# A two-layer mixer block on one core: the output gate's rows are made beside the attention

## The chip, the cores and the metric

The kernel runs on one core of one Trainium2 chip. Its engines are TensorE (in the profile PE for matmuls and PEld for weight loads), VectorE (DVE), ScalarE (ACT), GpSimd (POOL) and SyncE (SP), whose queue issues the transfers. The metric is the device time of one execution in microseconds (us), lower is better; given is the median of several runs.

## What is computed

Two layers of a block with 1024 latent tokens and 256 context tokens of width 1024. In each layer the tokens are normalised and modulated, projected, and pass four mixers (two kinds of attention, a state-space scan, a long convolution); the concatenated mixers are projected by `w_out`, normalised, scaled and added to the input:

```python
out_l = jnp.concatenate([a_l, g_l, s_l, y_l], axis=-1) @ w_out[l]
x = x + gt_l * rms_norm(out_l, g_post[l])
if need_ctx:                                  # layer 0 alone
    out_c = jnp.concatenate([a_c, g_c, s_c, y_c], axis=-1) @ w_out[l]
    ctx = ctx + gt_c * rms_norm(out_c, g_post[l])
```

`gt_l` and `gt_c` are the gate thirds of a modulation, `silu(c) @ w_mod[l] + b_mod[l]`, one row of 1024 numbers each. The kernel works with the product of gate and norm weight, `gt * g_post`, spread over the 128 partitions: one such row set for the latent tokens, and in layer 0 a second for the context tokens.

## The kernel before

The program is unrolled: two layers, each with filters and in-projection, scan and convolution, attention, out-projection. A planner orders the instructions of each engine's queue by program order and by when it expects their inputs, and gives each pool of tiles its memory; pools are stacked from the left or from the right side of the memory, and a new pool may take the place of one that was closed (with waits for the tiles that it overlaps). Matrix products are made as three products of halves with full rate: high by high, high by low, low by high (`whi`, `wlo`, `omh`, `oml`, `owh`, `owl`, and so on); a gate row is one product in full fp32.

The attention (`attention`) walks over units of one head and 256 queries: 40 in layer 0 (four pairs of heads, five query blocks, the last of them context), 32 in layer 1. Its instructions on TensorE, VectorE, ScalarE and GpSimd keep the order of the string `ORDER`, software-pipelined over units. The last step of each round, `X`, calls `pump()`, from the round of the first unit up to one round after the last unit. A call runs the products that the call before left in `self.later`, in the attention's fixed order, and then takes one more step of the generator `side`, whose instructions are outside the fixed order:

```python
late, self.later = self.later, []
for f in late:
    f()
self.token = None
more = next(side, self)
...
while pump():        # behind the last round
    pass
```

`side` (in `dit_kernel`) first makes the gate blocks of the modulation (`mod_gates`, 8 steps; they are stored to a DRAM tensor, `self.mg`, in the profile modg), in layer 0 then the modulation of layer 1 (`mod_next`, 16 steps), then opens the pool `wo` on the right side and loads and splits the out-projection's weights (`out_weights`, 16 steps, loads of [128, 512] under the tag `owr` with four buffers in the attention's pool). Each modulation step leaves four small products in `self.later`; they write a PSUM tile `mps` of the tag `f`, which the attention's transposes use too.

After the attention the pool `op` opens on the left side, in layer 0 above the pool `hp` of the next layer's inputs, in layer 1 at its bottom. At its head stand the gate rows: `gate_rows` loads the four partial rows from modg and the bias (`mg`, 5 x 1024), loads the norm's weight to all partitions (`gt`, 512 KB), sums and spreads the rows by two products into a PSUM tile (`gps`, of the tag that the scores and the out-projection use too), and multiplies (`gt`). Then `outproj` runs over tiles of 128 tokens (10 in layer 0, 8 in layer 1): it loads the mixers' output (`omx`, from mixD, which the attention's units store to) and their gates (`ogt`, from gD), multiplies them on VectorE, splits (`omh` on ScalarE, `oml` on GpSimd), makes 48 products `ops`, takes the square sum on ScalarE and `ors` from it, multiplies `ops`, `ors` and `gt` on VectorE into `oy`, adds the residual `oxt` on GpSimd and stores. In layer 0 each pair of tiles is also normalised for layer 1 (`xps`, `h`, `hh`, `hl`). At the last tile the pool `wo` is closed; after layer 0 the pool `wp` of layer 1's in-projection weights (`wraw`, `whi` on ScalarE, `wlo` on GpSimd, products `ipc`) opens on the right side, where `wo` lay.

All loads and stores are issued by SP's queue in order (line 201); TensorE's products come from line 224, transposes from line 253.

Of the kernel before, what the change touches and what calls it, by code (L numbers as in the profile page):

```python
# [11 lines left out]
F32 = mybir.dt.float32  # L12
# [8 lines left out]
ADD, SUB, MUL = ALU.add, ALU.subtract, ALU.mult  # L21
# [166 lines left out]
class K:  # L188
# [201 lines left out]
                    self.later.append(partial(put, blk, ms))  # L390
                yield

    def gate_rows(self, l, which, P, gD):

        A = self.A
        mg = P.tile([5, 1024], F32, tag="oy", name="mg", bufs=4)
        self.load(mg[0:4, :], gD)
        self.load(mg[4:5, :], A["b_modg"][l])
        g = P.tile([128, 1024], F32, tag="gt", name="gt", bufs=2)
        self.load(g, A["g_post"][l].partition_broadcast(128))  # L400
        ps = self.b2("gps")
        for h in range(2):
            self.mm(ps[:, h * 512:(h + 1) * 512], self.sel[:, which:which + 1].to_broadcast([5, 128]),
                    mg[:, h * 512:(h + 1) * 512])
        self.tt(g, ps, g, MUL)
        return g


    def load_x(self, dst, i):
# [1407 lines left out]
def dit_kernel(ctx: ExitStack, tc: tile.TileContext, A, out):  # L1817
    k = K(tc, A, out)
# [5 lines left out]
    for l in range(2):  # L1824
        need = l == 0
        n = 1280 if need else 1024
# [17 lines left out]
        with k.pool("fil", side="right") as F, k.pool("pol") as Q:  # L1844
# [42 lines left out]
            for c in SCRIPT[l]:  # L1887
                if c in blocks:
                    x = blocks[c]
# [44 lines left out]
        def side(R):  # L1934
            with k.pool("ma", side="right") as M:
                gates, cols = [(l, 4), (l, 5)], [(1, b) for b in range(4)] if l == 0 else []
                steps = partial(k.mod_steps, M, k.mod_feed(M, gates + cols))
                yield from k.mod_gates(l, steps)
                if cols:
                    yield from k.mod_next(1, steps, M)  # L1940
            O = wo.enter_context(k.pool("wo", side="right"))
            yield from k.out_weights(l, O, R)


        with k.pool("att") as W, k.pool("asl") as L, k.pool("ast") as P:
            k.attention(l, (W, L, P), n, side(W))
        w = k.wo
# [7 lines left out]
        with k.pool("op") as P:  # L1955
            def getx(t, i):
                if l == 0:
                    k.load_x(t, i)
                else:
                    k.load(t, xD[:, i])  # L1960

            def putx(t, i):
                k.store(xD[:, i] if l == 0 else ot[i], t)

            tiles = range(10 if need else 8)
            gt = [k.gate_rows(l, x, P, k.mg) for x in range(2 if need else 1)]
            xns = []
            for i in tiles:
                y, ps = k.outproj(l, P, i, w, gt[i // 8], getx, putx)
                if i == tiles[-1]:  # L1970
                    wo.close()
                if l == 0:
                    k.xn_tile(P, y, y, ps)
                    xns.append(y)
                    if len(xns) == 2:
                        k.norm_cols(P, (i - 1, i), xns, *k.mod, k.hh, k.hl)
                        xns = []
# [22 lines left out]
```

## Time and profile before

| | |
|---|---|
| runs, median of 3 | 2194.62 us (2193.89 to 2198.0) |
| the profiled execution | 2194.1 us |
| its span, first to last instruction | 2192.3 us |
| TensorE busy (matmuls) | 1937.6 us, 88% |
| VectorE busy | 1593.3 us, 73% |
| GpSimd busy | 992.0 us, 45% |
| ScalarE busy | 916.5 us, 42% |
| mean granted TensorE clock | 0.927 |

The attention of layer 0 lies at about 726 to 1066 us of the span, its out-projection at 1066 to 1217, layer 1's attention at 1820 to 2078, its out-projection from 2078 to the end. In a timeline row stand the start in us, the time from the first start to the last end of the merged instructions, the engine, the line, the operation, what is written and read, the count, and in brackets the engine's idle time ahead of it with what ended it. SPq rows are transfers being issued; their landing shows in who waits for them.

### The profile page before, as it was taken

The numbers are of one execution on the slowest core, as the hardware profiler recorded it, in microseconds if no ns is written. First come the engines' busy times: TensorE is split into PE (matmuls) and PEld (weight loads), VectorE is DVE, ScalarE is ACT, GpSimd is POOL, SyncE is SP. The second block draws the span as 40 slices with busy tenths as digits, with TensorE's granted clock in tenths as the row PEclk, the third lists the DMA queues.
The fourth block names the chain that finished last, engine by engine and source line by source line (L and its number), as shares of the span: only waits on it lengthen the run. The fifth ranks groups of instructions, "written<-read, shape, count | busy, mean of one in ns | idle before, by whom it ended". The sixth has DMA issues, their size and how long they took to land.

```text
span 2192.3 us, 31534 instructions
## 1 busy us (share of the span) xinstructions
PE 1937.6 (88%) x10811; PEld 1617.4 (74%) x10811; DVE 1593.3 (73%) x2982; ACT 916.5 (42%) x1958; POOL 992.0 (45%) x798
## 2 busy tenths in 40 slices
PE   5788998789899899999799998997989949999888
PEld 2577887678778777788577776886767737899866
DVE  8799439855896589789444598389577858999732
ACT  4421233224334467667322322343233317788611
POOL 3757225564661244432155557246675622340034
PEclk7798899899999899999799987998999979999989
DMA  6323365337765546352343423264357673551053
GB/s 222 115 88 119 129 203 142 92 115 212 237 186 183 159 127 180 101 149 69 114 156 113 151 100 144 86 232 145 98 173 221 202 231 100 137 159 54 21 176 131
DMA packets 261249, 316.55 MB, mean 144 GB/s; under 512 B 46655, under 2 KB 203583, under 8 KB 257762
## 3 DMA queue, kind: packets, MB, share of 16 engines
q1 hardware_dynamic: 261090, 314.55, 47.0%
q8 instruction: 85, 1.39, 0.3%
q14 instruction: 74, 0.61, 0.1%
HBM read 207.61 MB, written 106.86 MB: 143 GB/s over the span
## 4 chain that ended last, share of the span: by engine, by line
PE 44%; DVE 29%; DMA 10%; issue 6%; POOL 5%; SPq 3%; ACT 2%; POOLq 0%; DVEq 0%; ACTq 0%
PE ipc L224 8%; PE apo L224 7%; PE ops L224 6%; PE aS L224 6%; PE apt L253 6%; DVE lU L233 3%; DVE sD L233 3%; SPq L201 3%; PE acx L224 2%; DVE sp L233 1%; PE mps L224 1%; DMA aq<-gP 1%; DVE aPl L233 1%; DVE lX L233 1%; PE fdft L224 1%
## 5 line engine op out<-in xcount | busy, mean ns | idle before, releaser
L224 PE MATMUL ipc<-hh,whi 128*128 128x512 f32 (+2 forms) x992 | 386.6, 390 | 18.8 <-DVE rs L512 6.9
L224 PE MATMUL ipc<-hl,whi 128*128 128x512 f32 (+2 forms) x992 | 380.9, 384 | 1.6 <-POOL hl L233 1.6
L224 PE MATMUL ipc<-hh,wlo 128*128 128x512 f32 (+2 forms) x992 | 379.8, 383 | 0.3 <-POOL wlo L233 0.3
L233 DVE TENSOR_TENSOR aPl<-apt,aPh 128x512 fp32r<-128x512 f32 x328 | 224.0, 684 | 20.9 <-ACT aPh L1663 17.0
L1663 ACT CAST aPh<-apt 128x512 fp32r<-128x512 f32 x328 | 186.5, 590 | 123.4 <-PE apt L253 115.4
L233 POOL TENSOR_TENSOR wlo<-wraw,whi 128x512 fp32r<-128x512 f32 x108 | 162.6, 1510 | 161.2 <-ACT whi L453 158.5
L224 PEld LDWEIGHTS ipc<-hh,whi 128*128 128x128 f32 x992 | 196.4, 198 | 51.9 <-DVE rs L512 7.9
L224 PEld LDWEIGHTS ipc<-hh,wlo 128*128 128x128 f32 x992 | 196.3, 198 | 30.9 <-issue 1.8
L224 PEld LDWEIGHTS ipc<-hl,whi 128*128 128x128 f32 x992 | 196.8, 198 | 29.9 <-POOL hl L233 2.3
L253 PE MATMUL apt<-ident,aP 128*128 128x128 f32 x1312 | 190.6, 276 | 1.0 <-DVE aPl L233 1.0
L224 PE MATMUL aS<-kst,aq 128*128 128x512 f32 x512 | 153.7, 423 | 20.5 <-DMA aq<-gP 14.9
L1628 DVE TENSOR_REDUCE am<-aS 128x1 f32<-128x1024 f32 x128 | 155.6, 1216 | 15.0 <-PE aS L224 15.0
L1691 POOL COPY aLB<-am 128x128 f32<-128x128 f32 x72 | 21.0, 291 | 313.6 <-DVE am L1683 313.6
L246 ACT ACTIVATE aP<-aS,am,rs 128x1024 f32<-128x1024 f32 x128 | 155.6, 1215 | 15.3 <-DVE am L243 14.2
L253 PEld LDWEIGHTS apt<-ident,aP 128*128 128x128 f32 x1312 | 149.1, 141 | 14.8 <-DVE aPl L233 6.4
L224 PE MATMUL apo<-aPh,vst 128*128 128x256 f32 x656 | 138.2, 308 | 14.9 <-ACT aPh L1663 9.0
L224 PE MATMUL apo<-aPl,vst 128*128 128x256 f32 x656 | 123.8, 286 | 3.0 <-DVE aPl L233 2.9
L224 PEld LDWEIGHTS apo<-aPh,vst 128*128 128x128 f32 x656 | 96.4, 190 | 29.9 <-DVE aob L233 14.8
L453 ACT CAST whi<-wraw 128x512 fp32r<-128x512 f32 x124 | 75.4, 618 | 101.9 <-PE ipc L224 56.6
L224 PEld LDWEIGHTS aS<-kst,aq 128*128 128x128 f32 x512 | 88.7, 194 | 35.5 <-issue 15.8
L224 PE MATMUL ops<-owh,omh 128*128 128x512 f32 x288 | 94.4, 408 | 19.4 <-ACT omh L1776 13.6
L224 PEld LDWEIGHTS apo<-aPl,vst 128*128 128x128 f32 x656 | 100.3, 190 | 10.0 <-DVE aPl L233 5.3
(368 smaller groups left out, 4485.7 us busy)
## 6 DMA issues: line engine op xcount, KB each, us to landing
wraw<-in_w_col_dram SPq DMA_DIRECT2D x64, 256.0 KB, 2.9
mraw<-in_w_mod_dram SPq DMA_DIRECT2D x32, 512.0 KB, 5.3
kst<-mK SPq DMA_DIRECT2D x16, 640.0 KB, 10.8
omx<-mixD SPq DMA_DIRECT2D x18, 512.0 KB
ogt<-gD SPq DMA_DIRECT2D x18, 512.0 KB, 4.6
wraw<-in_w_mod_dram SPq DMA_DIRECT2D x32, 256.0 KB, 4.0
k<-kt SPq DMA_DIRECT2D x16, 512.0 KB
lk<-k SPq DMA_DIRECT2D x8, 1024.0 KB, 6.1
```

The lines of the kernel that those rows point to most:

```text
L201: return self.nc.sync.dma_start(out=out, in_=in_)
L224: self.keep(self.nc.tensor.matmul(out, lhsT, rhs, start=start, stop=stop))
L233: self.keep((eng or self.nc.vector).tensor_tensor(out=out, in0=a, in1=b, op=op))
L246: self.keep(self.nc.scalar.activation(out=out, in_=in_, func=func, **k))
L253: self.keep(self.nc.tensor.transpose(out, in_, self.ident[:p, :p]))
L453: self.nc.scalar.copy(hi, raw)
L1628: self.keep(nc.vector.tensor_reduce(out=x["m"][:, 2 + qi:3 + qi], in_=x["S"][qi], axis=AX.X, op=ALU.max))
L1663: self.keep(nc.scalar.copy(h, ps))
L1691: self.keep(nc.gpsimd.tensor_copy(x["LB"][:, :, o:o + 64], x["m"][:, 10:12].unsqueeze(2).to_broadcast([128, 2, 64])))
```

## The change

`gate_rows` becomes a part of `side`, behind `out_weights`. The rows are tiles of the pool `wo` now, one for each of `n` row sets (two in layer 0, one in layer 1), and are made in halves of 512 columns. Each half loads its piece of modg and of the bias into a buffer of the tag `owr`, and leaves one product of TensorE and one of VectorE in `self.later`, with a PSUM tile of the tag `f`. The head of the out-projection has no gate rows any more, and its pool has no tiles `gt` and `mg`.

```diff
-    def gate_rows(self, l, which, P, gD):
+    def gate_rows(self, l, n, P, R):
 
         A = self.A
-        mg = P.tile([5, 1024], F32, tag="oy", name="mg", bufs=4)
-        self.load(mg[0:4, :], gD)
-        self.load(mg[4:5, :], A["b_modg"][l])
-        g = P.tile([128, 1024], F32, tag="gt", name="gt", bufs=2)
-        self.load(g, A["g_post"][l].partition_broadcast(128))
-        ps = self.b2("gps")
-        for h in range(2):
-            self.mm(ps[:, h * 512:(h + 1) * 512], self.sel[:, which:which + 1].to_broadcast([5, 128]),
-                    mg[:, h * 512:(h + 1) * 512])
-        self.tt(g, ps, g, MUL)
-        return g
+        self.gt = []
+        for which in range(n):
+            g = P.tile([128, 1024], F32, name=f"gt{which}")
+            self.load(g, A["g_post"][l].partition_broadcast(128))
+            self.gt.append(g)
+            for h in (slice(0, 512), slice(512, 1024)):
+                mg = R.tile([5, 512], F32, tag="owr", name="mg", bufs=4)
+                self.load(mg[0:4, :], self.mg[:, h])
+                self.load(mg[4:5, :], A["b_modg"][l][:, h])
+
+                def put(which=which, g=g, h=h, mg=mg):
+                    ps = self.f("gps")
+                    self.mm(ps, self.sel[:, which:which + 1].to_broadcast([5, 128]), mg)
+                    self.tt(g[:, h], ps, g[:, h], MUL)
+
+                self.later.append(put)
+                yield
...
             yield from k.out_weights(l, O, R)
+            yield from k.gate_rows(l, 2 if need else 1, O, R)
...
-            gt = [k.gate_rows(l, x, P, k.mg) for x in range(2 if need else 1)]
             xns = []
             for i in tiles:
-                y, ps = k.outproj(l, P, i, w, gt[i // 8], getx, putx)
+                y, ps = k.outproj(l, P, i, w, k.gt[i // 8], getx, putx)
```

## Rows read from the trace of the kernel before

**Rows 1.** The page, part 4: shares of the chain that ended last, by engine.

```profile
PE 44%; DVE 29%; DMA 10%; issue 6%; POOL 5%; SPq 3%; ACT 2%; POOLq 0%; DVEq 0%; ACTq 0%
```

**Rows 2.** Windows: stretch, length, busy us of PE, PEld, DVE, ACT, POOL, clock, DMA.

```profile
1080.00:1217.00 137.00, 125.38 (x546) 99.37 (x545) 57.75 (x96) 37.79 (x64) 76.19 (x53) 0.96 0.44 138
...
1820.00:2078.00 258.00, 253.48 (x1790) 226.25 (x1789) 238.71 (x431) 204.50 (x438) 59.22 (x76) 1.00 0.36 96
...
2091.00:2192.00 101.00, 91.53 (x384) 73.12 (x383) 31.47 (x37) 15.64 (x23) 43.34 (x24) 0.96 0.46 146
```

**Rows 3.** Timeline of SP's queue, end of layer 0's attention.

```profile
1014.43 1.90 SPq L201 DMA_DIRECT2D aq<-mS  x4
1029.51 30.28 SPq L201 DMA_DIRECT2D mixD<-aob  x3
1059.84 0.33 SPq L201 DMA_DIRECT2D mg<-modg  x1
...
1066.76 0.35 SPq L201 DMA_DIRECT2D mixD<-aob  x1
...
1068.88 0.61 SPq L201 DMA_DIRECT2D ogt<-gD  x1
```

**Rows 4.** Timeline of all engines, head of layer 0's out-projection.

```profile
1065.71 7.39 PE L224 MATMUL gps<-mg,sel 5*128 5x512 f32 x8
...
1077.02 1.36 DVE L236 SCALAR_TENSOR_TENSOR omx<-omx,ogt 128x512 f32<-128x512 f32 x3 [6.27 <-DMA ogt<-gD]
...
1078.41 1.04 ACT L1776 CAST omh<-omx 128x1024 fp32r<-128x1024 f32 x1 [12.66 <-DVE omx L236]
...
1079.51 1.22 PE L224 MATMUL ops<-owh,omh 128*128 128x512 f32 x2 [6.42 <-ACT omh L1776]
```

**Rows 5.** Timeline of all engines, head of layer 1's out-projection.

```profile
2078.59 0.28 SPq L201 DMA_DIRECT2D mg<-modg  x1
...
2079.27 0.36 SPq L201 DMA_DIRECT2D gt<-in_g_post_dram  x1
2079.80 0.55 SPq L201 DMA_DIRECT2D omx<-mixD  x1
...
2080.76 2.78 PE L224 MATMUL gps<-mg,sel 5*128 5x512 f32 x4 [3.84 <-DMA mg<-in_b_modg_dram]
...
2088.18 1.36 DVE L236 SCALAR_TENSOR_TENSOR omx<-omx,ogt 128x512 f32<-128x512 f32 x3 [3.12 <-DMA ogt<-gD]
...
2090.68 1.22 PE L224 MATMUL ops<-owh,omh 128*128 128x512 f32 x2 [7.14 <-ACT omh L1776]
```

**Rows 6.** Timeline of all engines, from layer 0's last tile to layer 1's in-projection.

```profile
1214.30 6.69 SPq L201 DMA_DIRECT2D wraw<-in_w_col_dram  x4
...
1218.11 2.53 POOL L233 TENSOR_TENSOR wlo<-wraw,whi 128x512 fp32r<-128x512 f32 x2
...
1218.18 1.28 DVE L236 SCALAR_TENSOR_TENSOR oy<-ops,ors,gt 128x1024 f32<-128x1024 f32 x1 [2.11 <-POOL ors L233]
...
1219.45 0.80 PE L224 MATMUL ipc<-hh,wlo 128*128 128x512 f32 x1 [0.26 <-POOL wlo L233]
...
1220.57 2.41 POOL L233 TENSOR_TENSOR oy<-oy,oxt 128x1024 f32<-128x1024 f32 x1
```

**Rows 7.** Windows around layer 0's gate products and its first tile.

```profile
1068.90:1072.40 3.50, 3.50 (x5) 1.16 (x4) 1.23 (x1) 0.00 (x0) 0.00 (x0) 0.50 0.64 207
...
1084.90:1087.00 2.10, 2.10 (x10) 1.68 (x10) 0.00 (x0) 0.65 (x1) 1.37 (x1) 0.96 0.60 167
```

**Rows 8.** Timeline of POOL in layer 1's attention: its copy comes once a unit.

```profile
1847.11 0.29 POOL L1691 COPY aLB<-am 128x128 f32<-128x128 f32 x1 [2.17 <-DVE am L1683]
...
1881.62 0.29 POOL L1691 COPY aLB<-am 128x128 f32<-128x128 f32 x1 [2.17 <-DVE am L1683]
...
1929.63 0.29 POOL L1691 COPY aLB<-am 128x128 f32<-128x128 f32 x1 [1.52 <-DVE am L1683]
...
1945.18 0.29 POOL L1691 COPY aLB<-am 128x128 f32<-128x128 f32 x1 [1.75 <-DVE am L1683]
```

## The prediction

> **What bounds the kernel now.** I read the chain of work that ended last first: TensorE carries 44% of it, VectorE 29%, waits for transfers 10% [rows 1]. The kernel has several stages with different limits, so I split the span next. In the layer-1 attention TensorE is busy 253.5 us of 258 and VectorE 238.7; in the out-projection of layer 0 TensorE is busy 125.4 us of 137, in that of layer 1 91.5 of 101 [rows 2]. All three are bound by TensorE, so an instruction added to its stream in the attention costs its full time, and a head start of an out-projection is kept to its end. What the change touches is the few microseconds before an out-projection's first product. There the reader is to look at which wait ends last. In layer 0 the first product `ops` starts at 1079.51, after the cast omh at 1078.41, after the VectorE product that waited until 1077.02 for the load ogt [rows 4]; this load was issued on SP's queue at 1068.88, behind the loads of both gate rows, and landed 8.1 us later [rows 3]. In layer 1 it is the same: VectorE is released by ogt at 2088.18, first product at 2090.68 [rows 5]. The gate products themselves (gps) end before ogt lands and stand on no path: 1073.1 against 1077.0 in layer 0, 2083.5 against 2088.2 in layer 1 [rows 4, 5]. So what the change can win is not the products but their loads, which stand ahead of ogt on SP's queue and share the transfer engines with it.
>
> **What the change does, part by part.** The number of TensorE records of the gate rows stays at 12. The VectorE products become 6 halves instead of 3 wholes, the loads 15 instead of 9 (five for each set of rows: the norm's weight, and two for each half).
>
> *Where the work lands* follows from the code. The side generator is advanced once for each attention unit from the first on, and once after the last: 41 times in layer 0 (40 units), 33 times in layer 1 (32 units). Ahead of the gate rows it yields 8 + 16 + 16 = 40 times in layer 0 and 8 + 16 = 24 times in layer 1. So in layer 0 the first gate row comes up at the 41st and last call, and its four products are issued in the drain loop behind the attention: there the change moves only loads. In layer 1 both products run inside the attention.
>
> *Layer 0, head of the out-projection: 5.0 us won.* The loads of the rows need no attention tile, and SP has nothing but stores to wait for between its last query loads (the row of 1014.43 ends at 1016.3) and 1059.8 [rows 3]; I cost these ten loads at nothing, with that idle time as cover. If the cover were gone they would stand where they stand now. Before the change the first load of the out-projection's pool went out at 1059.84, ahead of the last store of the attention at 1066.76 [rows 3]. I read this as a wait for the attention's memory under that pool, not for the store. Now the first loads of that pool are omx and ogt, and I expect them in that place: ogt issued near 1060.5, landed by 1068.6 even at the 8.1 us of before, hidden beneath the last attention units. Then the next thing that is late is the gate products, which keep their place behind the attention's last transpose: 8 records of 512 columns at half clock, 0.85 us each (512 columns in two passes at 1.2 GHz; before, 7.39 us with a wait of some 0.5 us inside [rows 4]), from 1065.8 to 1072.6. The first `ops` product then starts at 1072.6, 6.9 us earlier. If VectorE has the last gate half (0.7 us) and the three products omx (1.36 us) behind that, and ScalarE the cast (1.04 us) [rows 4], it starts at 1075.7, 3.8 us earlier. If omx and ogt stay behind the last store, ogt goes out at 1067.7, lands in 5.9 us (two thirds of the 8.8 us that three such transfers take in layer 1, below) to 8.1 us, and with omx and omh behind it the gain is 1.3 to 3.5 us. I take 5.0 us, bounds 1.3 to 6.9.
>
> *Hand-over to layer 1: 3.5 us lost.* The rows now lie in the pool of the out-projection's weights (`wo`), which is closed at the last tile; the pool of layer 1's in-projection weights (`wp`) opens where it lay. Until now the last reader of `wo` was the last `ops` product, and the first weights' loads (wraw) went out right behind it at 1214.30 [rows 6]. Now the last reader is the VectorE product with the gate row at 1218.18, 3.9 us later. The loads themselves may still be issued at 1214.3, since they overlap the old weights and not the rows, but the order of the queues is fixed when the program is planned, and there they come after that product. On POOL the residual's addition, which is ready as soon as VectorE ends, then stands ahead of the splitting of the weights (wlo) instead of behind two of these: 1219.46 + 2.41 = 1221.87, and the first wlo is ready at 1221.87 + 1.26 = 1223.1, against 1219.4 now, when the first wlo product starts at 1219.45 [rows 6]. That is 3.7 us, and TensorE has few products that do not need wlo. Bounds: 0, if the loads and splits keep their order, and 7 us, if the second weights' cast also falls behind the square of the last tile on ScalarE. I take 3.5 us.
>
> *Layer 1, attention: 1.8 us lost.* Two products are added to a TensorE-bound stream. The four records took 2.78 us at the head, at a clock that was between the levels [rows 5]; at full clock a record of 512 columns in two passes is 0.43 us, so 1.7 us for both. The nearest row for what a put costs whole: units of the same kind with modulation products (four records of one pass) come every (1881.62 - 1847.11) / 4 = 8.63 us, those without every (1945.18 - 1929.63) / 2 = 7.78 us [rows 8], 0.85 us for 4 records. VectorE adds 0.7 us beside this. Bounds 0 (VectorE's and TensorE's small gaps take it) to 3 us (the PSUM buffer that it borrows from the transposes holds these up); 1.8 us.
>
> *Layer 1, head: 3.0 us won.* omx goes out where mg did, 2078.59 instead of 2079.80: 1.2 us [rows 5]. The 512 KB of the norm's weight leave the transfer engines: from its issue at 2079.27 to the landing of ogt at 2088.1 three transfers of 512 KB (weight, omx, ogt) take 8.8 us, of which a third is 2.9 us; part of the 8.8 us is latency that stays, so I take 1.8 us. Together 3.0 us, bounds 1.2 (the queue alone) and 4.1 us. Nothing else is late there: the gate products are gone from the stretch.
>
> One rule speaks against this. The rows show TensorE at 0.50 of its clock during the layer-0 gate products, though it was busy in all of 1068.9 to 1072.4, and at 0.96 only from 1084.9, 5.4 us after the first `ops` product [rows 4, 7]: the products did not raise the clock to 2.4 GHz, and so the out-projection starts at 1.2 GHz with them or without. The Trainium skill, "TensorE: Matmul & The Clock Gate" (section "HAM oscillation — how this bites in real kernels"), says that gaps between bursts of products throw the engine back to the low clock; by it, taking products out of the gap at layer 1's head would cost up to another half of those 5.4 us, 2.7 us, and the time would be 2194.6. The rows do not bear this out here.
>
> **The sum.** The profiled execution took 2194.1 us (span 2192.3). 2194.1 - 5.0 + 3.5 + 1.8 - 3.0 = 2191.4; the median of the runs lies 0.5 us above that execution, so 2191.9.
>
> **The rivals.**
> A hand-over without a price. For it: the first weights' loads waited for the last product alone. Against it: the first load of the out-projection's pool waited from 1016 to 1059 though SP was idle [rows 3], which looks like pools being released as a whole. Then -5.0 + 1.8 - 3.0 = -6.2: 2188.4; with the whole 6.9 us at layer 0's head 2186.5. This is faster by more than 0.2%.
> The loads do not move in layer 0: the change does not do what it says there. omx and ogt stay behind the last store and the gate products, late, gate them; the gain is 1.3 us, the hand-over is paid: -1.3 + 3.5 + 1.8 - 3.0 = +1.0: 2195.6. For it: the products are behind the attention in any case. Against it: the place at 1059.84 that three loads already had.
> A slower kernel: the hand-over at its whole price. On ScalarE the square of the last tile, which waits for POOL's addition, stands ahead of the second weights' cast, and layer 1 starts 7 us late; it decides once this price is above what both heads win less the attention's 1.8 us. With the heads at 1.3 and 1.2: -1.3 + 7 + 1.8 - 1.2 = +6.3: 2200.9; with the heads as forecast +0.8.
>
> **How the numbers follow.** 0.2% is 4.4 us, about what a measurement of this kernel can tell from no change. My forecast, 2191.9, has 0.45; the free hand-over 0.3; the loads that stay 0.13; the full price 0.12. The queues of the whole layer 1 are planned anew, so each case is some 3 us wide. The range is 2183.5 to 2201: from the free hand-over with the larger gain, 2186.5, less those 3 us, to the full price. Faster by over 0.2% (below 2190.2): the free hand-over and a quarter of the forecast, 0.4. Slower (above 2199.0): 0.12. Within: 0.48.
>
> **What would show it.** Right: on SP of layer 0 omx and ogt ahead of the last store of mixD, the first `ops` product at 1072 to 1076; gps in layer 0 still behind alb; in layer 1 two units longer by 0.9 us and ogt landing near 2085 less the shift; on POOL the last oy addition ahead of wlo, and TensorE idle for some 3 us more before the first wlo product. Wrong: if the weights of layer 1 split as early as now, or if stages that the change does not touch move by more than 3 us.

## The result, and the profile after

The changed kernel takes 2176.8 us (median, 2169.45 to 2181.21) beside 2196.3 us for the kernel before; the ratio is 0.9911, with an interval of 0.9896 to 0.9927. That is 19.5 us faster, 15 us below the prediction and outside its range. The profiled execution took 2180.56 us, its span is 2178.8 us. TensorE is busy 1941.8 us of it, VectorE 1591.4, and the chain of waits has nearly the shares of [rows 1]:

```profile
PE 44%; DVE 29%; DMA 10%; issue 7%; POOL 4%; ACT 3%; SPq 2%; POOLq 0%; DVEq 0%; ACTq 0%
```

Such shares do not tell where 19.5 us went. What tells it is to cut both spans at the same instructions and to compare the pieces. The cuts are GpSimd's first and last copy aLB in an attention, the first and last `ops` of an out-projection, and the first and last `sglu` (two products for each half block of the scan's last step). Single pieces of one and the same order of instructions differ by up to 3.4 us between executions (third line, the two profiles of the changed kernel); the first piece alone, in which no instruction differs, took 751.5 to 760.6 us in the profiles used here.

| piece, us (from the start of the first to the end of the last, read from the profiles) | before | after | after, second profile | layer 0 alone | layer 1 alone |
|---|---|---|---|---|---|
| layer 0: first aLB to first ops | 328.0 | 321.1 | 321.0 | 321.1 | 327.1 |
| layer 0: first to last ops | 135.2 | 135.3 | 135.5 | 135.3 | 133.7 |
| last ops to layer 1's first sglu | 556.8 | 552.1 | 555.5 | 551.2 | 556.0 |
| first to last sglu | 41.0 | 32.7 | 32.7 | 32.3 | 40.3 |
| last sglu to first aLB | 10.2 | 10.4 | 10.4 | 10.2 | 10.2 |
| layer 1: first to last aLB | 251.3 | 254.2 | 253.6 | 252.5 | 253.4 |
| last aLB to first ops | 16.7 | 13.2 | 13.3 | 15.3 | 13.3 |

The first, sixth and seventh line are the heads and the attention that the prediction speaks of. The fourth is a stage that the change does not touch, and it holds the largest gain.

The windows of layer 0's out-projection, layer 1's attention and layer 1's out-projection answer [rows 2] (stretch, length, busy us of PE, PEld, DVE, ACT, POOL, clock, DMA). All three are bound by TensorE as before:

```profile
1080.00:1217.00 137.00, 125.74 (x546) 99.03 (x545) 58.35 (x97) 37.77 (x63) 75.83 (x52) 0.96 0.44 137
1799.40:2064.20 264.80, 259.99 (x1806) 229.88 (x1806) 243.73 (x440) 209.68 (x447) 65.98 (x80) 1.00 0.39 104
2077.40:2178.50 101.10, 91.42 (x384) 73.29 (x384) 24.71 (x37) 15.65 (x23) 42.51 (x24) 0.96 0.46 146
```

SP's queue at the end of layer 0's attention, against [rows 3]. Up to here this execution is some 7 us later than that of before, in instructions that are the same:

```profile
1023.99 0.28 SPq L201 DMA_DIRECT2D mg<-modg  x1
...
1037.08 30.28 SPq L201 DMA_DIRECT2D mixD<-aob  x3
1067.72 0.55 SPq L201 DMA_DIRECT2D omx<-mixD  x1
1068.32 0.66 SPq L201 DMA_DIRECT2D ogt<-gD  x1
...
1073.64 0.33 SPq L201 DMA_DIRECT2D mixD<-aob  x1
```

omx and ogt stand where mg stood, ahead of the last store. The head of the out-projection, against [rows 4]:

```profile
1072.02 0.63 PE L253 MATMUL alb<-ident,aLB 128*128 128x128 f32 x2
...
1072.58 7.19 PE L224 MATMUL gps<-mg,sel 5*128 5x512 f32 x8
...
1077.00 1.35 DVE L236 SCALAR_TENSOR_TENSOR omx<-omx,ogt 128x512 f32<-128x512 f32 x3
...
1078.39 1.04 ACT L1782 CAST omh<-omx 128x1024 fp32r<-128x1024 f32 x1 [5.76 <-DVE omx L236]
...
1079.70 1.22 PE L224 MATMUL ops<-owh,omh 128*128 128x512 f32 x2
```

The products `gps` still stand behind the attention's last transpose, and `ops` follows them with no idle time; before, TensorE was idle for 6.42 us there. In layer 1 the head has no `gps` (against [rows 5]):

```profile
2068.34 0.32 SPq L201 DMA_DIRECT2D mixD<-aob  x1
2068.84 0.55 SPq L201 DMA_DIRECT2D omx<-mixD  x1
2069.48 0.62 SPq L201 DMA_DIRECT2D ogt<-gD  x1
...
2077.43 1.22 PE L224 MATMUL ops<-owh,omh 128*128 128x512 f32 x2 [10.28 <-ACT omh L1782]
```

The hand-over to layer 1, against [rows 6]: GpSimd adds the last residual ahead of the first wlo, and TensorE waits for that.

```profile
1214.53 0.82 SPq L201 DMA_DIRECT2D wraw<-in_w_col_dram  x2
...
1218.85 1.28 DVE L236 SCALAR_TENSOR_TENSOR oy<-ops,ors,gt 128x1024 f32<-128x1024 f32 x1 [2.55 <-POOL ors L233]
...
1220.22 2.34 POOL L233 TENSOR_TENSOR oy<-oy,oxt 128x1024 f32<-128x1024 f32 x1 [1.40 <-DVE oy L236]
1222.51 1.27 POOL L233 TENSOR_TENSOR wlo<-wraw,whi 128x512 fp32r<-128x512 f32 x1
...
1223.83 0.80 PE L224 MATMUL ipc<-hh,wlo 128*128 128x512 f32 x1 [3.54 <-POOL wlo L233]
```

GpSimd's copy in the two units of layer 1 that hold the products, against [rows 8]: 9.93 and 8.90 us for a unit, where the units of before at this place took 8.56 and 7.77.

```profile
2014.27 0.29 POOL L1697 COPY aLB<-am 128x128 f32<-128x128 f32 x1 [7.48 <-DVE am L1689]
2024.20 0.30 POOL L1697 COPY aLB<-am 128x128 f32<-128x128 f32 x1 [9.64 <-DVE am L1689]
2033.10 0.30 POOL L1697 COPY aLB<-am 128x128 f32<-128x128 f32 x1 [8.60 <-DVE am L1689]
```

So far each change stands in the queues where the forecast has it. The gain that it does not have lies between layer 1's in-projection and its attention. There the scan's last step runs over four blocks of 256 tokens: load two pairs sgy and sgg (128 KB each), make sz on VectorE, multiply (`sglu`), make sth on ScalarE and VectorE, store it to mixD. The attention's first product `acx` follows the last `sglu`. SP's queue and TensorE in the kernel before:

```profile
1791.54 0.54 SPq L201 DMA_DIRECT2D owr<-in_w_out_dram  x1
1792.18 0.85 SPq L201 DMA_DIRECT2D mixD<-sth  x2
1793.12 1.38 SPq L201 DMA_DIRECT2D mraw<-in_w_mod_dram  x3
1794.55 2.49 SPq L201 DMA_DIRECT2D owr<-in_w_out_dram  x3
1797.14 0.52 SPq L201 DMA_DIRECT2D sgy<-yD  x1
...
1800.74 0.32 SPq L201 DMA_DIRECT2D sgg<-uD  x1
```

```profile
1793.58 2.69 PE L224 MATMUL sglu<-sz,sgw 128*128 128x256 f32 x8
1808.98 3.51 PE L224 MATMUL sglu<-sz,sgw 128*128 128x256 f32 x8 [12.71 <-DVE sz L236]
1812.47 0.73 PE L224 MATMUL acx<-kst,aq 128*128 128x256 f32 x4
```

And in the changed kernel:

```profile
1788.93 0.53 SPq L201 DMA_DIRECT2D sgy<-yD  x1
...
1790.50 0.38 SPq L201 DMA_DIRECT2D sgg<-uD  x1
...
1791.61 1.02 SPq L201 DMA_DIRECT2D owr<-in_w_out_dram  x2
...
1795.26 1.54 SPq L201 DMA_DIRECT2D mraw<-in_w_mod_dram  x3
```

```profile
1795.91 3.78 PE L224 MATMUL sglu<-sz,sgw 128*128 128x256 f32 x8 [4.45 <-DVE sz L236]
```

Before, the last block's loads go out behind four loads of the out-projection's weights (owr, 256 KB each) and three of the modulation's (mraw, 512 KB each), 2.5 MB that nobody needs before the attention has begun; after the change they go out ahead of them. The planner made another order of layer 1's queues.

### The profile page after: what moved, and what is told of

It is laid out like the page before. It is cut to its first block, busy times and chain, and to the rows that moved or that the text cites. A ratio compares the mean times of both kernels' runs of the same rounds, so it can differ in the third digit from the quotient of the medians.

```text
span 2178.8 us, 31556 instructions
## 1 busy us (share of the span) xinstructions
PE 1941.8 (89%) x10811; PEld 1615.2 (74%) x10811; DVE 1591.4 (73%) x2985; ACT 917.5 (42%) x1958; POOL 1000.7 (46%) x798
## 4 chain that ended last, share of the span: by engine, by line
PE 44%; DVE 29%; DMA 10%; issue 7%; POOL 4%; ACT 3%; SPq 2%; POOLq 0%; DVEq 0%; ACTq 0%
PE ipc L224 8%; PE apo L224 7%; PE ops L224 6%; PE apt L253 6%; PE aS L224 6%; DVE lU L233 3%; DVE sD L233 3%; SPq L201 2%; DVE sp L233 2%; PE acx L224 2%; PE fdft L224 2%; PE mps L224 1%; DVE lX L233 1%; PE hps L224 1%; DMA px<-qkvD 1%
## 5 line engine op out<-in xcount | busy, mean ns | idle before, releaser
L246 ACT ACTIVATE aP<-aS,am,rs 128x1024 f32<-128x1024 f32 x128 | 155.7, 1217 | 15.3 <-DVE am L243 14.2
```

The source lines that it names most:

```text
L246: self.keep(self.nc.scalar.activation(out=out, in_=in_, func=func, **k))
```

## The experiments

**Which layer's edit.** Two kernels have the change in one layer alone:

```diff
             yield from k.out_weights(l, O, R)
-            yield from k.gate_rows(l, 2 if need else 1, O, R)
+            if l in LAYERS:            # (0,) or (1,)
+                yield from k.gate_rows(l, 2 if need else 1, O, R)
...
+            if l not in LAYERS:        # as before, at the head
+                k.gt = [k.head_rows(l, x, P, k.mg) for x in range(2 if need else 1)]
```

> The gate rows move beside the attention in layer 0 alone; layer 1 makes its rows at the head of the out-projection as before. Theory A (the gain comes from layer 0's head and from the new order of layer 1's queues between its in-projection and its attention, both consequences of layer 0's edit): layer 0's head wins 7.0 us against its attention's end, the first attention product acx of layer 1 starts some 20 us earlier than before against the start of layer 0's out-projection stage, and the whole is 19 to 20 us faster than the kernel before (ratio about 0.991). Rival B (layer 1's own edit brings the gain of the stage ahead of its attention): 7 us faster at most, less 4 for the hand-over, ratio 0.997 to 0.999.

> The gate rows move beside the attention in layer 1 alone; layer 0 is the kernel before, and up to layer 1's attention every engine has the order of before. Theory A: only the attention's two units (+2.5 to +2.9 us) and the head of the out-projection (-3.5 us) change: ratio 0.9995 to 1.000, no measurable difference; the scan's last product sglu in layer 1 ends near 1812 us as before. Rival B (layer 1's edit brings the gain ahead of its attention): 10 to 13 us faster, ratio about 0.995.

Measured: layer 0 alone 0.993 (0.9908 to 0.9952), layer 1 alone 1.0004 (0.9989 to 1.0018). The table above has their pieces. Layer 0's edit brings the 6.8 us at its own head and the shorter stage in layer 1 (32.3 us from first to last sglu); layer 1's brings 3.4 us at its head and costs 2.1 us in its attention, and the time stays the same. Theory A stands.

**The hand-over alone.** Only the two row tiles of layer 0 move into the weights' pool; the code that loads and multiplies stays at the head.

```diff
+            k.gt = [O.tile([128, 1024], F32, name=f"gt{x}") for x in range(2)] if l == 0 else [None]
...
-            gt = [k.gate_rows(l, x, P, k.mg) for x in range(2 if need else 1)]
+            gt = [k.gate_rows(l, x, P, k.mg, k.gt[x]) for x in range(2 if need else 1)]
```

> The kernel before, with layer 0's two row tiles placed in the pool of the out-projection's weights; loads, products and their place at the head are those of before. So the hand-over alone: the last reader of that pool is VectorE's product with the row. First wlo product of layer 1 some 4 us later than before (near 1223.5). Layer 1's queues come out in a third order, with the last pair of the scan's loads (sgy, sgg) behind the out-projection's and modulation's first weights, as before. Theory A (the place of that pair decides the stage): layer 1's stage ahead of its attention ends within 3 us of before; the whole 0 to 4 us slower, ratio 1.000 to 1.002. Rival C (the delayed hand-over itself gives layer 1 a better order): 8 to 13 us faster, ratio 0.994 to 0.996.

Measured: 1.0002 (0.9988 to 1.0016). The first wlo product comes 8.9 us after the last `ops` (1224.04 - 1215.17) against 4.7 before (1219.45 - 1214.73), so the delay of 4 us is there; but the filter's first product `fps` starts 39.4 us after the last `ops` against 39.9. In the kernel before TensorE runs 155 records between 1219.4 and 1254.6, here and in the changed kernel 134 in the same window: the in-projection's products are postponed, and the filters do not wait for them. The planner made a third order of layer 1 with the weights ahead of the last loads; sglu lasts 39.0 us.

The equal time does not by itself show that the hand-over is free, since this kernel differs from the one before in more than that. The planner moved layer 0's two loads of the norm's weight, whose tiles now lie in the weights' pool, out of the head to 961.89:

```profile
961.89 2.29 SPq L201 DMA_DIRECT2D gt<-in_g_post_dram  x2
1079.48 1.22 PE L224 MATMUL ops<-owh,omh 128*128 128x512 f32 x2 [3.37 <-ACT omh L1777]
```

TensorE is idle for 3.37 us ahead of the first `ops` instead of 6.42, and the head's piece lasts 324.4 us instead of 328.0. This gain of 3.6 us and 2.0 us in sglu stand against 3.8 us lost in the piece between (560.6 instead of 556.8 us). That loss is not the delay carried on, since the long convolution's products `ldft` in the middle of the piece end 501.9 us after the last `ops` against 513.6; it arises behind them, in the third order. So the delay is made good at `fps`; what the third order costs beside it is not separated.

**Waits inside the scan's last step.** The first reading was that one wait of this chain had gone. The next runs take waits away by more buffers, in layer 1 alone; in the first sgy and sgg have four, in the later ones sth too, by the same edit to its tile:

```diff
-                y = P.tile([128, 256], F32, tag="sgy", name="sgy", bufs=2)[:, :n]
-                g = P.tile([128, 256], F32, tag="sgg", name="sgg", bufs=2)[:, :n]
+                y = P.tile([128, 256], F32, tag="sgy", name="sgy", bufs=2 if l == 0 else 4)[:, :n]
+                g = P.tile([128, 256], F32, tag="sgg", name="sgg", bufs=2 if l == 0 else 4)[:, :n]
```

> The kernel before with one edit that has nothing to do with the gate rows: in layer 1 the scan's last step has four buffers instead of two for each of its loads sgy and sgg. The planner then puts the last pairs of these loads ahead of the attention's query loads and of the out-projection's and modulation's first weights, as in the changed kernel; TensorE's order is that of before up to the scan's last products. Theory A: the last product sglu ends 8 to 12 us earlier than in the kernel before, the attention starts that much earlier, and the whole is 8 to 12 us faster, ratio 0.9945 to 0.9965. Rival D (the stage was won by another order of TensorE's in-projection or of earlier steps): within 2 us of before, ratio 0.999 to 1.001.

Measured: 0.999 (0.9976 to 1.0005), less than theory A wanted and as rival D has it. But sglu lasts 36.2 us instead of 41.0, so the stage does depend on the loads, and rival D is settled further below. All loads are early now, but the weights still go out ahead of the results' stores, and ScalarE, which has two buffers for sth, waits for these:

```profile
1801.49 0.84 ACT L246 ACTIVATE sth<-sglu,sgb 128x256 f32<-128x256 f32 x2 [5.48 <-DMA mixD<-sth]
```

> The kernel before; in layer 1 the scan's last step has four buffers instead of two for its results sth, two as before for the loads sgy and sgg. The run with four load buffers won 4 to 5 us at this stage: the last block's wait for its loads went (VectorE's 7.5 us of idle time before the last block), and ScalarE then waited for the stores of sth instead (8.9 and 5.5 us). Theory E (the stage is a chain of four blocks with two waits that cover each other, the loads' place in SP's queue and the stores that free sth): here the waits of ScalarE for the stores go, but the last loads still stand behind the first weights and query loads, so that VectorE waits longer for them; sglu ends 0 to 5 us earlier than before, ratio 0.9975 to 1.000. Rival F (the stores alone hold the stage up): sglu ends 8 to 12 us earlier, ratio 0.9945 to 0.996.

Measured: 1.000 (0.9989 to 1.0012); sglu lasts 40.2 us, and VectorE waits for the loads twice instead (5.94 and 5.96 us). One wait alone gives nothing that the time shows, as theory E says.

> The kernel before; in layer 1 the scan's last step has three buffers instead of two for each of its loads and four instead of two for its results, so both waits of the chain are taken away together; nothing of the gate rows is touched. Theory E: the last sglu ends 10 to 16 us earlier than before, the attention starts that much earlier, ratio 0.993 to 0.996, about what the changed kernel won in this stage (13 us). Rival G (the gain of the stage is bound to another order of TensorE's in-projection, which is here that of before): at most 5 us, ratio above 0.9975.

Measured: 0.9971 (0.9959 to 0.9983). sglu lasts 30.9 us, 10.1 less than before, as expected; from the last sglu to the attention's first copy it is 12.8 us instead of 10.2, and the whole wins some 6 us, less than theory E expected and a little more than rival G allows. In this kernel's queue the weights stand behind the last loads too (sgg at 1790.50, mraw at 1792.94, owr at 1795.87).

> The changed kernel, with the same buffers for the scan's last step (three and four). Theory E: what is left of that chain in the changed kernel is ScalarE's wait of 5.2 us for the stores of sth and VectorE's of some 2 us for loads; the attention of layer 1 starts 4 to 7 us earlier than in the changed kernel, ratio to the kernel before 0.9875 to 0.990. If the stage is by now bound by the in-projection of TensorE, which ends 18 us before the attention starts, or by the attention's own loads: 0.990 to 0.992, no gain over the change.

Measured: 0.9918 (0.9903 to 0.9932), no gain over the change; sglu lasts 32.2 us. VectorE waits 7.72 us for a load sgg that now stands behind the attention's keys and values. The second case of the expectation holds.

> The changed kernel as it is, beside the others on the same chip: ratio 0.990 to 0.993. A second profile of it tells which shifts belong to the order of the queues and which to the one execution: head of layer 0's out-projection 7 us earlier against its attention's end, start of layer 1's attention 13 us earlier against the end of layer 0, in both profiles, within 1.5 us.

Measured: 0.991 (0.9894 to 0.9926). Layer 0's head is 7.0 us shorter again and sglu lasts 32.7 us again, but the attention starts 9.4 us earlier against layer 0's end, not 13: the piece ahead of the first sglu took 555.5 us instead of 552.1. So some 3 us of the first reading belonged to the one execution.

**The place in the queue, or the traffic.** If a place in SP's queue were all, the scan's loads on a queue of their own would win:

```diff
-                self.load(y, yD[:, hf, c])
-                self.load(g, uD[:, hf, c])
+                (self.nc.scalar if l else self.nc.sync).dma_start(out=y, in_=yD[:, hf, c])
+                (self.nc.scalar if l else self.nc.sync).dma_start(out=g, in_=uD[:, hf, c])
```

> The kernel before, buffers as before (two of each); in layer 1 the loads sgy and sgg of the scan's last step are issued from ScalarE's queue instead of SP's, so that they no longer stand behind the attention's query loads and the first weights. TensorE's order is that of before up to the last products sglu. Theory E (place in SP's queue, then the stores that free sth): the scan's finish, first sglu to last, shortens from the 41 us of before by the 4 to 8 us of VectorE's wait for the last loads, while ScalarE's wait for the stores of sth (8.6 us) stays: ratio 0.9965 to 0.998. If the loads' place did not matter and only the traffic on the transfer engines did, the stage stays as long as before: ratio 0.999 to 1.001.

Measured: 1.000 (0.9986 to 1.0013); sglu lasts 39.4 us. Theory E's 4 to 8 us do not come. But the loads now stand among ScalarE's own instructions, and the last four went out 22.6 to 26.4 us after the first sglu, against 25.7 to 29.3 before: some 3 us earlier. The last sgy landed 6.89 us after its issue, against 5.53 before. TensorE's order is not quite that of before either: it differs from the first sglu on. So the run does not tell the place from the traffic. The Trainium skill, "DMA: Bandwidth & Descriptors" (section "Issuing engines are not separate DMA queues"), says that transfers issued by different engines run on the same 16 transfer engines and interleave there; this run's 1.000 agrees, but could not show it alone.

> The changed kernel with the same edit: the scan's loads on ScalarE's queue, two buffers each. In the changed kernel they already stand ahead of the first weights, and VectorE waits some 2 us for the last. Theory E: 0 to 3 us faster than the changed kernel, ratio to the kernel before 0.989 to 0.991; the finish lasts 30 to 33 us (32.7 in the changed kernel).

Measured: 0.9954 (0.9937 to 0.9971): half of the change's gain is lost. sglu lasts 39.5 us, about as before the change, and the attention's first copy comes 14.3 us behind it instead of 10.4. SP no longer waits for the scan's buffers ahead of the attention's first loads, and these go out some 3 us earlier against the first sglu (1765.35 here, 1767.03 in the changed kernel): the second load of the keys at 6.2 us instead of 9.6, the values at 8.0 instead of 11.5, the first query load at 8.9 instead of 12.1. The scan's last loads go out later, 25.6 to 28.8 us after the first sglu instead of 21.9 to 23.5, and behind the weights owr, whose own place is nearly the same (24.0 instead of 24.6):

```profile
1789.31 1.35 SPq L201 DMA_DIRECT2D owr<-in_w_out_dram  x3
1790.92 0.33 ACTq L1334 DMA_DIRECT2D sgy<-yD  x1
...
1794.17 0.33 ACTq L1335 DMA_DIRECT2D sgg<-uD  x1
```

That the waits in SP's queue had been a brake on the attention's loads, and that these now slow the scan's small transfers on the transfer engines, fits these times; it is argued, not shown, since ScalarE's order is a rival cause for the late issue.

> The changed kernel with the scan's loads on ScalarE's queue and three buffers for each of them, four for the results: no wait for a place in SP's queue and none for the stores. With SP's queue alone these buffers won nothing (ratio 0.9918 against 0.991), because VectorE then waited 7.7 us for loads that stood behind the attention's keys. Theory E: this wait goes, the finish lasts 24 to 29 us, the attention of layer 1 starts 3 to 8 us earlier than in the changed kernel, ratio 0.987 to 0.9895. Rival (the attention's own first loads, or the traffic, are late next): 0.990 to 0.992.

Measured: 0.9923 (0.9909 to 0.9937); sglu lasts 34.0 us. With more buffers the loss is made good, but nothing is won over the change; theory E's 24 to 29 us do not come, and the ratio is near the rival's.

**The weights alone.** The last theory (H) is that the transfer engines carry 2.5 MB too early. The windows from first to last sglu show them busy 0.82 of the time at 242 GB/s before and 0.91 at 256 GB/s after (last two columns), so 9.9 MB in the longer window and 8.3 MB in the shorter one:

```profile
1771.50:1812.50 41.00, 15.28 (x43) 10.69 (x43) 16.05 (x36) 8.29 (x20) 6.67 (x4) 0.63 0.82 242
```

```profile
1767.00:1799.40 32.40, 24.09 (x86) 18.10 (x84) 15.27 (x38) 9.25 (x22) 0.00 (x0) 0.82 0.91 256
```

At the 242 GB/s of before, 2560 KB would take 10.8 us, as an estimate. The edit holds these loads, and only these, behind the last sz; TensorE's and GpSimd's orders are exactly those of the kernel before:

```diff
                 self.stt(z[:, hf], g, 1.0, y, ADD, MUL)
+                if l == 1 and c0 == 768:
+                    self.nc.vector.tensor_copy(self.mark, z[:, hf, 0:1])
...
+                if self.hold and len(held) < ahead + 1:        # layer 1, first buffers of mraw and owr
+                    held.append(t)
+                    self.nc.vector.tensor_copy(t[:, 0, 0:1] if len(shape) > 2 else t[:, 0:1], self.mark)
                 self.load(t, src)
```

> The kernel before; in layer 1 the first loads of the modulation's and the out-projection's weights (mraw, three of 512 KB, and owr, four of 256 KB, 2.5 MB together) are held until VectorE has made the scan's last block sz, by a copy of one column into each buffer ahead of its load. TensorE's and GpSimd's orders are exactly those of before; the buffers and the queue of the scan's loads too. Theory H (the stage is bound by the transfer engines, busy 0.82 of it at 242 GB/s before and 0.91 at 256 GB/s in the changed kernel; the changed kernel is shorter because these 2.5 MB go out behind the scan's last loads instead of ahead of them): the finish, first sglu to last, shortens from 41 us to 31 to 36 us, the attention starts 5 to 10 us earlier, ratio 0.9955 to 0.998. Theory E (one place in a queue or one buffer is late) has no reason left after its loads on a queue of their own won nothing; it gives the same only if the last loads alone decide. Rival I (TensorE's order of the in-projection, which ends 11 us later against the scan in the changed kernel): no gain, ratio 0.999 to 1.001.

Measured: 0.9963 (0.995 to 0.9976). sglu lasts 30.8 us, 10.2 less than before, and the transfer engines are busy 0.74 of it at 207 GB/s. The last loads go out at 1793.67 to 1795.03, the weights from 1800.98:

```profile
1795.03 0.38 SPq L201 DMA_DIRECT2D sgg<-uD  x1
1798.45 1.19 SPq L201 DMA_DIRECT2D mixD<-sth  x2
1800.98 1.28 SPq L201 DMA_DIRECT2D mraw<-in_w_mod_dram  x3
1802.37 0.37 SPq L201 DMA_DIRECT2D owr<-in_w_out_dram  x1
```

```profile
1800.02 2.85 PE L224 MATMUL sglu<-sz,sgw 128*128 128x256 f32 x8 [2.54 <-DVE sz L236]
1802.59 1.22 PE L224 MATMUL acx<-kst,aq 128*128 128x256 f32 x4
```

TensorE waits 2.54 us for the last sz instead of 12.71, with nothing of the gate rows changed. This is the gain of the untouched stage, made by itself: the weights' loads ahead of the scan's last loads are its cause. Rivals D and I fall, since TensorE's order is that of before.

Whether the weights hurt by their place in SP's queue or by their traffic, the trace answers with both. The row of VectorE's two products on the last loads, before, and of the second of them, with the weights held:

```profile
1804.79 2.25 DVE L236 SCALAR_TENSOR_TENSOR sgy<-sgg,sdd,sgy 128x256 f32<-128x256 f32 x2 [7.54 <-DMA sgg<-uD]
```

```profile
1797.40 0.48 DVE L236 SCALAR_TENSOR_TENSOR sgy<-sgg,sdd,sgy 128x256 f32<-128x256 f32 x1 [0.35 <-DMA sgg<-uD]
```

The last load sgg goes out 23.0 us after the first sglu instead of 29.3 (1795.03 - 1772.03, 1800.74 - 1771.48), and VectorE's product with it starts 2.4 us after its issue instead of 5.8 (1797.40, 1806.57). So 6.3 us of the 10.2 are an earlier issue and 3.5 us a shorter way from issue to use. How far the transfers in flight also delay the issue is not separated, and theory E's place in the queue is not refuted.

> The changed kernel with the same hold on the first weights. Here they stand behind the scan's last loads already, so theory H expects nothing: the finish lasts 32 to 34 us (32.7 without), ratio to the kernel before 0.990 to 0.992. A gain of more than 4 us over the changed kernel would say that the weights slow down the scan's stores too.

> The changed kernel with the hold and with three buffers for each of the scan's loads, four for its results: an attempt at a faster version. Theory H: with the weights behind, what is left ahead of the attention is the scan's own traffic and the attention's first keys, values and queries; 0 to 5 us faster than the changed kernel, ratio 0.9885 to 0.991.

Measured: in the changed kernel the hold gives 0.993 (0.9912 to 0.9947), a little above the expected ratio, and sglu lasts 32.6 us, so nothing is left to win there by it, as H says. With the buffers as well it is 0.9905 (0.989 to 0.992) and 29.9 us, not to be told from the change alone (0.9911). No version beat it measurably.

## Why the prediction was wrong, step by step

*Layer 0's head.* Forecast 5.0 us, bounds 1.3 to 6.9; measured 6.9 (328.0 to 321.1). The path was right: omx and ogt in mg's place, the products behind the attention, these late next. I took a middle value because VectorE's last gate half might stand ahead of omx; the trace has it at 1079.81, behind all three omx, and the cast ends 0.3 us ahead of the products (1079.43, 1079.77). One reading on the way was wrong: SP was not free ahead of 1059.84, and mg had no wait of its own there. The three stores of mixD stood ahead of it in SP's queue, each waiting for its unit, and mg, now omx, comes right behind the third.

*Hand-over.* Forecast a loss of 3.5 us; the first wlo product is 4.2 us later against the last `ops`, by the place on GpSimd that was named. The step that failed here is the one from there to the end. I carried the wait into the sum at full price because TensorE has few products without wlo. It does wait, but 35 us later the filters' first product is not late (39.5 us after the last `ops` in the changed kernel, 39.9 before), since the filters start from other inputs. A wait costs only what it makes the work behind it late.

*Layer 1, attention.* Forecast a loss of 1.8 us; measured 2.3 and 2.9 in the two profiles (2.1 with layer 1's edit alone). The term was a little too small: the two units lost 2.5 us together.

*Layer 1, head.* Forecast 3.0 us; measured 3.5 and 3.4. The kernels without layer 1's edit took 15.3 to 17.1 us here and those with it 13.2 to 14.0, so single differences are good to about 1 us. The rule of the Trainium skill, "TensorE: Matmul & The Clock Gate" ("HAM oscillation — how this bites in real kernels"), that spoke against it brought no added cost: TensorE now idles 10.28 us ahead of the first `ops` instead of 7.14 and starts at 1.2 GHz, as it did before (granted clock 0.51 in the first 4.3 us, 0.52 in the first 5.0 before), and the pairs of products reach 0.63 us 4.3 us after the first one (2081.68), against 5.0 before (2095.64).

Put together, with the hand-over at nothing, these steps give -6.9 + 2.6 - 3.5 = -7.8 us, near 2187, which is the rival with the free hand-over. The rest was not in any case.

*The stage that the change does not touch.* This is the larger failed step: the term for the new plan of layer 1's queues, which the prediction put at nothing in the sum and at some 3 us in the range, without a reason for that size. The text named the test that it then failed: wrong if untouched stages move by more than 3 us. The new plan brought 8.3 to 8.7 us between first and last sglu in the three profiles of the table with layer 0's edit, 0.7 us in that with layer 1's alone, and weights_held shows the cause. With it the steps give -16.1 us of the 19.5. I did not look for the stage of layer 1 that hung on the planner's order. It could be seen in the trace of before: TensorE idle for 12.71 us of 15.4 ahead of the last sglu, and ahead of the loads that VectorE waited for, on SP's queue, seven loads that nobody needed yet. The width for the new plan should have been that wait, mostly to the faster side, since the order of before was bad at this place.

What stays open: the piece ahead of the first sglu was 1.3 to 5.5 us shorter in the three profiles of the table with layer 0's edit. Over all kernels it took 548.9 to 555.5 us with that edit (median 552.1 of eight) and 553.4 to 557.1 us where layer 1 is planned nearly as before (median 556.2 of seven). So some 4 us of it probably belong to the new order too; which work gains them was not traced. And why the planner put the weights behind the loads is argued, not shown: their buffers lie where the in-projection's inputs and weights lay, and the in-projection ends 14.8 us after the first sglu in the changed kernel against 3.3 before (1781.8 - 1767.0, 1774.8 - 1771.5). In handover_only it is 3.0 us, with the weights ahead.

## What to carry to other kernels

An edit in a kernel whose queues a planner orders is also a new throw for all stages behind it; before summing the edit's own terms, go through the later stages for a long wait that hangs on the order of transfers, and make the range as wide as that wait. When a stage that you did not touch moves, move the suspected transfers alone, with every other engine's order kept, and see if the gain comes without the edit. Loads that are free to go early are not free if small transfers of the critical stage are under way.

## What was not expected of the hardware

More buffers on one side or a queue of their own for the waiting loads won next to nothing (0.999, 1.000, 1.000), while 2560 KB of weights, held until the scan's last block was made, won 10.2 us in the same stage. With them under way VectorE could use the last load of 128 KB 5.8 us after its issue, without them after 2.4 us. A queue of their own even cost some 10 us in the changed kernel (0.9954 against 0.991): the scan's last loads then went out 3.7 to 5.3 us later than on SP's queue, and the attention's first loads some 3 us earlier.
